# A gated-linear-attention layer with a convolutional FFN on one core: VectorE's order in the opening fixed, side work moved to other units, the last LayerNorm moved behind the first FFN iteration

## The chip, the cores and the metric

The kernel runs on one core of one Trainium2 chip. Its metric is the device time of one execution in microseconds (us). Three runs of the kernel before took 2148.79, 2154.12 and 2155.0 us; their median is 2154.12 us. The execution that the profiler recorded took 2152.2 us.

## What is computed

One decoder layer on 2048 tokens of width 1024, in float32. First a token mixer, gated linear attention in 4 heads (key width 128, value width 256, chunks of 64 tokens), then a gated FFN (inner width 2816) with a causal depthwise convolution of width 3. Each of the two is modulated by a conditioning vector c (shift, scale, gate) and followed by a residual and a LayerNorm:

```python
cs = jax.nn.silu(c)
shift, scale, gate = jnp.split((cs @ w_mod + b_mod)[:, None, :], 3, axis=-1)
y = sublayer(x * (1 + scale) + shift)
x = layer_norm(DN_ALPHA * x + (1 + gate) * y, ln_gain, ln_bias)
# sublayer 1
q, k, v, r, a_lr = jnp.split(h @ w_in, [qk, 2 * qk, 2 * qk + dv, 2 * qk + 2 * dv], axis=-1)
log_a = jax.nn.log_sigmoid((a_lr @ w_a2 + b_a).astype(jnp.float32)) / GLA_TAU
# S_t = diag(a_t) S_(t-1) + k_t^T v_t, o_t = q_t S_t, then norm, * silu(r), @ w_o
# sublayer 2
u, g = jnp.split(h @ w_up, 2, axis=-1)
return (jax.nn.silu(conv(u)) * g) @ w_down
```

## The kernel before

Every float32 operand of a matmul is split into a high and a low part, x = hi + lo. The high part is a cast by ScalarE (ACT, L107), the low part a subtraction by VectorE (DVE, L110). A product is three matmuls of TensorE (PE): hi·hi, hi·lo, lo·hi (mm3, L113 to L115). So each tile that PE is to multiply passes ScalarE and VectorE first.

The program has these stages, by the trace: the opening (0 to 60.6 us), four token blocks of 512 tokens each for the mixer (to 875.9 us), 44 iterations of the FFN's up product (22 column groups for each of two halves of the tokens), and the down product, which ends at 2142.1 us; a tail follows.

*Opening.* Shift and scale for x are needed first. For each pair pr of k-tiles (two tiles of 128 of the 1024 input channels), VectorE sums c-weighted rows of the modulation matrix (mod_cols: one pass of ScalarE and seven of VectorE over macc, L233), four small matmuls against ones turn the sum into a column (mod_fin, L242), and VectorE adds the bias (md, L243). Then x of this pair is modulated (make, L529), split into xm, and multiplied with the weight units of q, k, v and with the decay weights (waw, L508 and L509). A weight unit is 512 KB of raw weights, split into a tile hl. Until then PE runs matmuls on a constant tile (spin, L423).

*Token blocks.* A block goes through units of weights; at_unit(u, f) runs a side step f when unit u is taken. Such side steps are gate_step (a column of a gate, summed over rows by VectorE), x_pre (sums of tokens for the FFN), make_xm (modulating x of the next block, L385), next_decays, ln1_out (LayerNorm output, transposed) and the first weights of the FFN. Heads are worked in pairs: K is scaled by decays into KI (L637) and decayed again by VectorE (L641), PE transposes it (L658), and then multiplies Q with KI and v with the transposed KTt. After the block follows out_proj (L753) with its LayerNorm: bn_stats and bn_aggr on VectorE, one over the root on POOL (L173, L174, L802), the normalisation on ScalarE (normalise, L803).

*FFN.* The up product is done by seven products of sums of tiles (prod), like Strassen's. x for these lies in tiles xc, weights are summed on VectorE (L319). A result in PSUM is copied out by ScalarE (keep: p1, u2, u3; L941) before the next product of the same bank may change it, so a late copy holds up PE.

*Tail.* The last down product ends with an eviction by VectorE, the sum of squares by ScalarE (L1186), one over the root on POOL (L1193, L1194) and two rounds of y (L1191, L1197), then the stores.

A scheduler sets the order of each engine's instructions when the program is built; order(a, b) fixes that a comes after b on the same engine, without a wait. An engine runs its instructions strictly in that order, so one that waits holds up all behind it. DMAs are issued by SyncE's queue (SP).

## Time and profile before

| | before |
|---|---|
| median of three runs | 2154.12 us |
| profiled execution | 2152.2 us |
| its span, first to last instruction | 2150.5 us |
| mean granted TensorE clock | 0.997 |
| PE busy | 2129.3 us (99%) |
| VectorE busy | 1428.9 us (66%) |
| ScalarE busy | 890.3 us (41%) |
| POOL busy | 116.9 us (5%) |

Busy time is time in which an engine ran instructions. PE's matmuls are pipelined, so a record of 0.39 us follows another after about 0.23 us. A row of the timeline gives the start, the time and the instruction, with xN where N equal ones follow each other; the bracket at the end is the idle time before it and what ended it. The granted clock is a share of TensorE's full speed of 2.4 GHz.

### The profile page before, as it was taken

The numbers are of one execution on the slowest core, as the hardware profiler recorded it, in microseconds if no ns is written. First come the engines' busy times: TensorE is split into PE (matmuls) and PEld (weight loads), VectorE is DVE, ScalarE is ACT, GpSimd is POOL, SyncE is SP. The second block draws the span as 40 slices with busy tenths as digits, with TensorE's granted clock in tenths as the row PEclk, the third lists the DMA queues.
The fourth block names the chain that finished last, engine by engine and source line by source line (L and its number), as shares of the span: only waits on it lengthen the run. The fifth ranks groups of instructions, "written<-read, shape, count | busy, mean of one in ns | idle before, by whom it ended". The sixth has DMA issues, their size and how long they took to land.

```text
span 2150.5 us, 26695 instructions
## 1 busy us (share of the span) xinstructions
PE 2129.3 (99%) x9909; PEld 1773.2 (82%) x9909; DVE 1428.9 (66%) x2001; ACT 890.3 (41%) x1346; POOL 116.9 (5%) x266
## 2 busy tenths in 40 slices
PE   9999999999999999999999999999999999999998
PEld 7888888888888888788888888888888888888886
DVE  7786676434743453777877778776666796578556
ACT  4655443424242333644444445333333443344333
POOL 0010100010001000100000000000000000021002
PEclk9999999999999999999999999999999999999999
DMA  8386887674866666767845559877777797577562
GB/s 301 117 320 218 321 324 275 220 252 174 294 228 254 250 237 231 268 225 283 313 175 185 184 210 326 307 256 265 258 270 266 270 333 262 194 239 257 192 203 88
DMA packets 154818, 529.28 MB, mean 246 GB/s; under 512 B 17632, under 2 KB 21856, under 8 KB 134464
## 3 DMA queue, kind: packets, MB, share of 16 engines
q1 hardware_dynamic: 154688, 527.58, 69.0%
q8 instruction: 78, 1.28, 0.2%
q14 instruction: 52, 0.43, 0.1%
HBM read 364.72 MB, written 162.79 MB: 245 GB/s over the span
## 4 chain that ended last, share of the span: by engine, by line
PE 91%; DMA 3%; DVE 2%; ACT 1%; issue 1%; POOL 0%; SPq 0%; DVEq 0%; POOLq 0%; ACTq 0%
PE ps_mm L113 22%; PE ps_mm L115 22%; PE ps_mm L114 22%; PE ps_w L114 8%; PE ps_w L113 8%; PE ps_w L115 8%; DMA mraw<-in_mws_dram 1%; PE ps_w L786 1%; PE ps_w L738 1%; DMA xs<-xm_d 0%; DMA xraw<-in_xT_dram 0%; DMA xs<-xt_d 0%; DMA graw<-in_mwg_dram 0%; PE ps_w L508 0%; DMA xp<-xm_d 0%
## 5 line engine op out<-in xcount | busy, mean ns | idle before, releaser
L113 PE MATMUL ps_mm<-xc,hl 128*128 128x512 f32 x704 | 274.5, 390 | 2.0 <-ACT hl L107 1.9
L115 PE MATMUL ps_mm<-xc,hl 128*128 128x512 f32 x704 | 274.3, 390 | 0.5 <-DVE hl L110 0.5
L114 PE MATMUL ps_mm<-xc,hl 128*128 128x512 f32 x704 | 274.1, 389 | 0.0
L113 PE MATMUL ps_mm<-xm,hl 128*128 128x512 f32 x496 | 194.9, 393 | 1.4 <-DVE v L110 1.4
L114 PE MATMUL ps_mm<-xm,hl 128*128 128x512 f32 x496 | 193.6, 390 | 0.0
L115 PE MATMUL ps_mm<-xm,hl 128*128 128x512 f32 x496 | 193.6, 390 | 0.0
L113 PEld LDWEIGHTS ps_mm<-xc,hl 128*128 128x128 f32 x704 | 132.3, 188 | 29.9 <-ACT hl L107 2.4
L115 PEld LDWEIGHTS ps_mm<-xc,hl 128*128 128x128 f32 x704 | 132.2, 188 | 28.5 <-DVE hl L110 1.0
L114 PEld LDWEIGHTS ps_mm<-xc,hl 128*128 128x128 f32 x704 | 132.2, 188 | 27.7 <-DVE xc L110 0.5
L955 DVE SCALAR_TENSOR_TENSOR ct<-U,cw_sb,ct 128x512 f32<-128x512 f32 x176 | 131.8, 749 | 19.3 <-ACT ct L949 17.8
L115 PE MATMUL ps_w<-xc,hl 128*128 128x512 f32 x352 | 136.9, 389 | 0.0
L113 PE MATMUL ps_w<-xc,hl 128*128 128x512 f32 x352 | 136.9, 389 | 0.0
L114 PE MATMUL ps_w<-xc,hl 128*128 128x512 f32 x352 | 136.9, 389 | 0.0
L107 ACT CAST dhl<-raw 128x1024 fp32r<-128x1024 f32 x57 | 60.2, 1056 | 165.6 <-PE ps_mm L115 101.5
L110 DVE TENSOR_TENSOR dhl<-raw,dhl 128x1024 fp32r<-128x1024 f32 x57 | 69.7, 1223 | 70.1 <-ACT dhl L107 70.1
L113 PEld LDWEIGHTS ps_mm<-xm,hl 128*128 128x128 f32 x496 | 93.2, 188 | 20.7 <-DVE v L110 1.8
L115 PEld LDWEIGHTS ps_mm<-xm,hl 128*128 128x128 f32 x496 | 93.2, 188 | 19.8 <-issue 0.2
L114 PEld LDWEIGHTS ps_mm<-xm,hl 128*128 128x128 f32 x496 | 93.3, 188 | 18.2 <-issue 0.2
L107 ACT CAST hl<-raw 128x1024 fp32r<-128x1024 f32 (+1 forms) x73 | 70.6, 969 | 88.4 <-PE ps_mm L115 41.2
L110 DVE TENSOR_TENSOR hl<-raw,hl 128x1024 fp32r<-128x1024 f32 (+1 forms) x73 | 81.4, 1117 | 36.6 <-ACT hl L107 36.0
L113 PE MATMUL ps_mm<-dhl 128*128 128x512 f32 x264 | 102.7, 389 | 0.0
L114 PE MATMUL ps_mm<-dhl 128*128 128x512 f32 x264 | 102.7, 389 | 0.0
(237 smaller groups left out, 4960.3 us busy)
## 6 DMA issues: line engine op xcount, KB each, us to landing
hl<-wq_d SPq DMA_DIRECT2D x82, 1024.0 KB, 4.9
hc_d<-ct SPq DMA_DIRECT2D x154, 256.0 KB, 2.7
raw<-hc_d SPq DMA_DIRECT2D x70, 512.0 KB, 4.3
draw<-wc_d SPq DMA_DIRECT2D x70, 512.0 KB, 4.7
wq_d<-hl SPq DMA_DIRECT2D x32, 1024.0 KB, 4.9
raw<-in_wab_dram SPq DMA_DIRECT2D x46, 512.0 KB, 6.4
wu<-in_wup_dram SPq DMA_DIRECT2D x44, 512.0 KB, 4.3
wg<-in_wup_dram SPq DMA_DIRECT2D x44, 512.0 KB, 3.7
```

Source lines behind the costliest of these rows:

```text
L107: accs["copy"] = nc.scalar.copy(h, src)
L110: return nc.vector.tensor_tensor(l, src if lsrc is None else lsrc, h.bitcast(F32), op=ALU.subtract)
L113: nc.tensor.matmul(po, a[0], b[0], start=first, stop=False, skip_group_check=resumed)
L114: nc.tensor.matmul(po, a[0], b[1], start=False, stop=False, skip_group_check=resumed)
L115: return nc.tensor.matmul(po, a[1], b[0], start=False, stop=last, skip_group_check=resumed)
L738: nc.tensor.transpose(pt[:, s * P:s * P + P], on[:, s, e * P:e * P + P], ident)
L786: nc.tensor.transpose(pt[:, t * P:t * P + P], src, ident)
L955: nc.vector.scalar_tensor_tensor(ct, U[:, o + i:o + i + 512], cw_sb[:, j, i:i + 1], ct, op0=ALU.mult, op1=ALU.add)
```

## The change

1. Opening: a list (seq) puts every VectorE instruction of the opening in one fixed order. The high parts of x come directly from ScalarE's modulating pass; VectorE computes the low part. For even k-tiles VectorE modulates a copy (xr) itself, for odd ones ScalarE makes a second pass. Two weight units are loaded ahead of x and not one. Each pair's products come in the order q and k, v, mod_fin of the next pair, decays. Twelve spin matmuls stand ahead of the second mod_fin.
2. gate_step of the first block is placed at units 10 to 15 and gate_end at 16, before at 12 to 19 and 20.
3. The modulation of the next block's x (make_xm) is ordered behind the latest decay pass on K.
4. In the last block x_pre comes at units 1 and 12 of the block, before at 4 and 13; the LayerNorm output of block 2 is read back from DRAM at units 14 to 17 of block 3.
5. Start of the FFN: one x tile is loaded at unit 25 of block 3, the others come in halves, two of them later; the last block's LayerNorm is written behind the first iteration.
6. Tail: the last LayerNorm takes bn_stats and bn_aggr (VectorE) and no sum of squares by ScalarE.

```diff
-SPIN = (64, 13)
+SPIN = (64, 8, 12)
...
-    def mod_fin(s, pr):
+    def mod_fin(s, pr, stand_in=None):
         acc = accs.pop((s, pr))
         pm = psum("w", 4)
+        if stand_in is not None:
+            stand_in(pm)
...
-                    nc.vector.tensor_scalar(r, r, md[:, 0, kt, 1:2], md[:, 0, kt, 0:1], op0=ALU.mult, op1=ALU.add)
+                    i = nc.vector.tensor_scalar(r, r, md[:, 0, kt, 1:2], md[:, 0, kt, 0:1], op0=ALU.mult, op1=ALU.add)
+                    order(i, accs["k"])
...
+        def seq(i):
+            if dve:
+                order(i, dve[-1])
+            dve.append(i)
+            return i
...
-        mod_cols(0, 0, range(4), start[0][0])
+        mod_cols(0, 0, range(4), start[0][0], seq=seq)
...
             def make(pr):
-                mm, i = mod_fin(0, pr)
+                mm, i = mod_fin(0, pr, (lambda pm: spin(SPIN[2], pm)) if pr == 1 else None)
+                seq(i)
                 if pr == 0:
-                    order(i, accs["hl"])
                     spin(SPIN[1], ps_spin, mm)
+                    seq(accs["hl"])
                 for kt in (2 * pr, 2 * pr + 1):
                     r = start[pr][1][:, kt % 2 * 512:kt % 2 * 512 + 512]
-                    if kt == 1:
-                        i = nc.vector.tensor_scalar(r, r, md[:, 0, kt, 1:2], md[:, 0, kt, 0:1], op0=ALU.mult, op1=ALU.add)
+                    t = act_tile("xm")
+                    b, a = md[:, 0, kt, 0:1], md[:, 0, kt, 1:2]
+                    hi = nc.scalar.activation(t[:, 0], r, AF.Identity, bias=b, scale=a)
+                    if kt % 2 == 0:
+                        rr = t2p.tile([P, 512], F32, tag="t2", name="xr")
+                        seq(nc.vector.tensor_scalar(rr, r, a, b, op0=ALU.mult, op1=ALU.add))
                     else:
-                        nc.scalar.activation(r, r, AF.Identity, bias=md[:, 0, kt, 0:1], scale=md[:, 0, kt, 1:2])
-                    if kt == 1:
-                        fw.append(unit())
-                        order(accs["hl"], i)
-                    t = act_tile("xm")
-                    sub = split(t[:, 0], t[:, 1], r)
+                        rr = r
+                        hi = nc.scalar.activation(r, r, AF.Identity, bias=b, scale=a)
+                    seq(nc.vector.tensor_tensor(t[:, 1], rr, t[:, 0].bitcast(F32), op=ALU.subtract))
                     xm.append(t)
-                return sub
+                return hi
...
             fw.append(unit())
-            done = make(0)
-            mod_row1(0, 1, start[1][0], accs["copy"])
-            accs["last"] = done
-            make_waw(done)
-            issue(3)
+            seq(accs["hl"])
+            fw.append(unit())
+            hi = make(0)
+            mod_row1(0, 1, start[1][0], hi)
+            split_unit(3, hi)
+            decay_w = make_waw()
+            hi = next(decay_w)
             for pr in range(4):
                 if pr < 3:
                     load_unit()
                     if pr < 2:
                         start_loads(pr + 2)
-                        mod_row1(0, pr + 2, start[pr + 2][0], accs["copy"])
-                    mod_cols(0, pr + 1, range(4), start[pr + 1][0], range(1, KT), accs["hl"] if pr == 0 else mod_done)
-                    mod_done = accs["last"]
-                for po, w in ((pq, fw[0]), (pk, fw[1])):
-                    wv = w.rearrange("p s (k c) -> p s k c", k=KT)
-                    for kt in (2 * pr, 2 * pr + 1):
-                        mm3(po, (wv[:, 0, kt], wv[:, 1, kt]), (xm[kt][:, 0], xm[kt][:, 1]), kt == 0, kt == KT - 1)
+                        mod_row1(0, pr + 2, start[pr + 2][0], hi)
+                    mod_cols(0, pr + 1, range(4), start[pr + 1][0], range(1, KT), seq)
+                if pr == 0:
+                    next(decay_w, None)
+                kts = (2 * pr, 2 * pr + 1)
+                views = [(po, w.rearrange("p s (k c) -> p s k c", k=KT)) for po, w in ((pq, fw[0]), (pk, fw[1]))]
+
+                def part(kt, a, b):
+                    for po, wv in views:
+                        nc.tensor.matmul(po, wv[:, a, kt], xm[kt][:, b], start=kt + a + b == 0,
+                                         stop=kt == KT - 1 and b == 1)
+
+                for kt in kts:
+                    part(kt, 0, 0)
+                    part(kt, 1, 0)
+                    if pr > 0:
+                        part(kt, 0, 1)
+                if pr == 0:
+                    for kt in kts:
+                        part(kt, 0, 1)
+                v_part(banks, pr, xm, pr == 0)
                 if pr < 3:
-                    accs["last"] = make(pr + 1)
-                mm_a(pa, xm, (2 * pr, 2 * pr + 1))
+                    hi = make(pr + 1)
+                    split_unit(4 + pr, hi)
+                mm_a(pa, xm, kts)
                 if pr == 2:
                     make_w2s()
-                if pr < 3:
-                    issue(4 + pr)
-                v_part(banks, pr, xm)
...
-            nc.vector.tensor_tensor(kk, kk, el[:, 1:3].rearrange("p c s -> p s c")[:, :, :, None].to_broadcast([P, 4, 2, CH]),
-                                    op=ALU.mult)
+            d = el[:, 1:3].rearrange("p c s -> p s c")[:, :, :, None].to_broadcast([P, 4, 2, CH])
+            accs["k"] = nc.vector.tensor_tensor(kk, kk, d, op=ALU.mult)
...
-                if half == 1:
-                    normalise(zs[t])
-                    store(zn_d[tb * 4 + t], zs[t])
+                if half == 1 and tb < NTB - 1:
+                    ln1(tb, t, zs)
             tick()
+
+        def ln1(tb, t, zs):
+            normalise(zs[t])
+            store(zn_d[tb * 4 + t], zs[t])
...
+            first["x"] = [raw_tile("xs") for pr in range(2)]
+            for pr in range(2):
+                load(first["x"][pr], xt_d[0][3][pr])
...
-                for k in range(8):
-                    at_unit(12 + k, gate_step, 0, k, gs1)
-                at_unit(20, gate_end, 0, G1, gs1)
+                for k, u in enumerate((10, 10, 11, 11, 11, 12, 14, 15)):
+                    at_unit(u, gate_step, 0, k, gs1)
+                at_unit(16, gate_end, 0, G1, gs1)
...
-                at_unit(b + 4, x_pre, 0, 0)
-                at_unit(b + 13, x_pre, 0, 1)
+                at_unit(b + 1, x_pre, 0, 0)
+                at_unit(b + 12, x_pre, 0, 1)
+                for pr in range(4):
+                    at_unit(b + 14 + pr, ln1_out, 2, None, (pr,))
...
-            if 0 < tb < NTB - 1:
+            if tb == 1:
...
+        def x_halves(i):
+            X0[i] = []
+            for pr in range(2):
+                t = x_tile(ur, i)
+                half, b = X_AT[i] if i < 4 else (0, 0)
+                for k in range(2):
+                    r = hid_tile("xs")
+                    load(r, xm2_d[b][2 * half + pr][:, k] if i < 3 else xt_d[0][i][pr][:, k * 512:k * 512 + 512])
+                    h = t[:, :, k * 512:k * 512 + 512]
+                    split(h[:, 0], h[:, 1], r)
+                    X0[i].append((h[:, 0], h[:, 1]))
+
+        x_halves(4)
...
-            if n == 0:
-                start_rest()
...
+            if n == 0:
+                x_fill(ur, X0, 3, first["x"])
...
+            if n == 0:
+                x_halves(2)
+                for t in range(4):
+                    ln1(NTB - 1, t, zs_last)
...
+    def ln2_last(p, b, t):
+        a, sm = acc.pop((p, b, t))
+        st = sts.pop()
+        nc.vector.bn_stats(st[:, 1], a[:, 512:1024])
+        mv = smp.tile([P, 2], F32, tag="mv", name="mv")
+        nc.vector.bn_aggr(mv, st)
+        rs = smp.tile([P, 2], F32, tag="rs", name="rs")
+        rsqrt_eps(rs[:, 0:1], mv[:, 1:2])
...
+            y = t2p.tile([P, 512], F32, tag="t2", name="y")
+            nc.vector.scalar_tensor_tensor(y, a[:, cs_], mv[:, 0:1], rows[2][half], op0=ALU.subtract, op1=ALU.mult)
...
+            nc.vector.scalar_tensor_tensor(ys[half], ys[half], rs[:, 0:1], rows[3][half], op0=ALU.mult, op1=ALU.add)
...
-                    ln2(p, b, t)
+                    ln2_last(p, b, t)
...
+                    sts.append(smp.tile([P, 2, 6], F32, tag="bst", name="bst"))
+                    nc.vector.bn_stats(sts[-1][:, 0], acc[p, b, t][0][:, 0:512])
```

How this moves instructions shows in the order of the two programs at three places. First VectorE in the opening, from the md of the second pair to that of the third; macc is the sum of modulation rows, xm the split x, hl a weight unit. Before:

```order
L243 TENSOR_TENSOR md<-ps_w,mbs_sb 128x4
L233 SCALAR_TENSOR_TENSOR macc<-mraw,cs,macc 128x512 x3
L110 TENSOR_TENSOR xm<-xraw,xm 128x512 x2
L233 SCALAR_TENSOR_TENSOR macc<-mraw,cs,macc 128x512
L110 TENSOR_TENSOR hl<-raw,hl 128x1024
L233 SCALAR_TENSOR_TENSOR macc<-mraw,cs,macc 128x512 x2
L243 TENSOR_TENSOR md<-ps_w,mbs_sb 128x4
```

and after the change, where xr is the modulated copy:

```order
L244 TENSOR_TENSOR md<-ps_w,mbs_sb 128x4
L556 TENSOR_SCALAR xr<-xraw,md 128x512
L560 TENSOR_TENSOR xm<-xr,xm 128x512
L560 TENSOR_TENSOR xm<-xraw,xm 128x512
L110 TENSOR_TENSOR hl<-raw,hl 128x1024
L233 SCALAR_TENSOR_TENSOR macc<-mraw,cs,macc 128x512 x7
L244 TENSOR_TENSOR md<-ps_w,mbs_sb 128x4
```

The passes over macc were spread around the splits of x and of the weights; now all splits of a pair stand in front of all seven passes for the next one. On PE, at the end of the second pair's work, before (L242 is mod_fin, hl,xm the v product):

```order
L115 MATMUL ps_mm<-hl,xm 128x512
L113 MATMUL ps_mm<-hl,xm 128x512
L242 MATMUL ps_w<-ones,macc 128x1 x4
L114 MATMUL ps_mm<-hl,xm 128x512
L115 MATMUL ps_mm<-hl,xm 128x512
```

and after (L243 is mod_fin, L521 and L522 the decay matmuls, L591 the next pair's q and k):

```order
L115 MATMUL ps_mm<-hl,xm 128x512
L522 MATMUL ps_w<-xm,waw 96x512
L521 MATMUL ps_w<-xm,waw 96x512
L522 MATMUL ps_w<-xm,waw 96x512
L243 MATMUL ps_w<-ones,macc 128x1 x4
L591 MATMUL ps_w<-xm,hl 128x512 x12
L113 MATMUL ps_mm<-hl,xm 128x512 x4
```

mod_fin stood among the v products of its pair and now stands behind the last matmul of the pair.

Second, the first head, on PE: behind the Q·KI matmuls, before:

```order
L114 MATMUL ps_w<-Q,KI 128x192
L115 MATMUL ps_w<-Q,KI 128x192
L114 MATMUL ps_mm<-xm,hl 128x512
L115 MATMUL ps_mm<-xm,hl 128x512
L113 MATMUL ps_mm<-xm,hl 128x512
```

and after:

```order
L114 MATMUL ps_w<-Q,KI 128x192
L115 MATMUL ps_w<-Q,KI 128x192
L113 MATMUL ps_w<-v,KTt 128x256
L114 MATMUL ps_w<-v,KTt 128x256
L115 MATMUL ps_w<-v,KTt 128x256
```

The product of v with KTt followed later and now follows at once. VectorE from the decay pass of the first head (KI_787) to KTt, after:

```order
L684 TENSOR_TENSOR KI_787<-KI_787,el 128x512
L667 SCALAR_TENSOR_TENSOR Q_823<-ps_mm,E_772 128x4x64
L110 TENSOR_TENSOR KI<-KI_860,KI 128x512
L668 TENSOR_TENSOR Q_823<-Q_823,el 128x4x64
L684 TENSOR_TENSOR KI_860<-KI_860,el 128x512
L110 TENSOR_TENSOR Q<-Q_823,Q 128x768
L110 TENSOR_TENSOR KTt<-ps_w,KTt 128x512
```

Six instructions stand from there to KTt's low part, one of them (KI of the second head, KI_860) in front of the second head's decay pass.

Third, ScalarE at the start of the FFN, where z is a LayerNorm tile, hl a weight unit, p1 and u2 are copies from PSUM and xc is x, before:

```order
L803 ACTIVATE z_7262<-z_7262,rs_7570 128x1024
L107 CAST h3_7616<-s3_7504 128x512
L803 ACTIVATE z_7264<-z_7264,rs_7582 128x1024
L107 CAST hl_7662<-wg_7345 128x1024
L941 COPY p1_7657<-ps_mm_7644 128x512
L803 ACTIVATE z_7266<-z_7266,rs_7594 128x1024
L803 ACTIVATE z_7268<-z_7268,rs_7606 128x1024
L107 CAST hl_7703<-wu_7640 128x1024
L941 COPY u2_7720<-ps_mm_7644 128x512
L107 CAST hl_7725<-wu_7640 128x1024
```

and after:

```order
L107 CAST hl_7653<-wg_7376 128x1024
L993 COPY p1_7648<-ps_mm_7635 128x512
L107 CAST xc_7611<-xs_7612 128x512
L107 CAST xc_7611<-xs_7616 128x512
L848 ACTIVATE z_7295<-z_7295,rs_7772 128x1024
L107 CAST xc_7620<-xs_7621 128x512
L107 CAST hl_7674<-wu_7631 128x1024
L107 CAST xc_7620<-xs_7625 128x512
L1001 ACTIVATE ct_7672<-U_7669,cb_sb_104,cw_sb_103 128x512
L107 CAST xc_7677<-xs_7379 128x1024
L107 CAST xc_7680<-xs_7380 128x1024
L993 COPY u2_7697<-ps_mm_7635 128x512
```

Two LayerNorm passes stand ahead of the cast of hl (hl_7703 before, hl_7674 now; the first of the two above these rows) where four stood, and the copy of u2, which followed it at once, now has three more casts and a convolution pass ahead of it.

## Rows read from the trace of the kernel before

**Rows 1.** The page's part 1: busy time, share, instructions of each engine.

```profile
PE 2129.3 (99%) x9909; PEld 1773.2 (82%) x9909; DVE 1428.9 (66%) x2001; ACT 890.3 (41%) x1346; POOL 116.9 (5%) x266
```

**Rows 2.** Waits of PE: engine line waited for, total us, times, longest us.

```profile
PE ps_w L658 <- DVE KI L641: 3.0, 3, 1.3
...
PE ps_mm L113 <- ACT hl L107: 1.9, 1, 1.9
PE ps_mm L113 <- DVE v L110: 1.4, 1, 1.4
...
PE ps_w L113 <- ACT v L107: 0.3, 1, 0.3
PE ps_w L114 <- DVE v L110: 0.3, 1, 0.3
```

**Rows 3.** Timeline, PE, opening: start us, us, engine line op, idle before.

```profile
15.53 0.73 PE L113 MATMUL ps_w<-xm,hl 128*128 128x512 f32 x2 [1.19 <-ACT xm L107]
...
24.68 1.05 PE L242 MATMUL ps_w<-ones,macc 128*128 128x1 f32 x8 [0.35 <-DVE macc L233]
...
28.50 1.22 PE L113 MATMUL ps_w<-xm,hl 128*128 128x512 f32 x2 [1.76 <-ACT xm L107]
...
60.59 0.63 PE L482 MATMUL ps_w<-A,w2s 96*128 96x512 f32 x2
```

**Rows 4.** Timeline, VectorE (DVE), opening.

```profile
26.23 0.16 DVE L243 TENSOR_TENSOR md<-ps_w,mbs_sb 128x4 f32<-128x4 f32 x1
26.35 2.33 DVE L233 SCALAR_TENSOR_TENSOR macc<-mraw,cs,macc 128x512 f32<-128x512 f32 x3
28.59 1.29 DVE L110 TENSOR_TENSOR xm<-xraw,xm 128x512 fp32r<-128x512 f32 x2
...
30.46 1.22 DVE L110 TENSOR_TENSOR hl<-raw,hl 128x1024 fp32r<-128x1024 f32 x1
```

**Rows 5.** Timeline, ScalarE (ACT), opening.

```profile
26.42 1.52 ACT L539 ACTIVATE xraw<-xraw,md 128x512 f32<-128x512 f32 x2 [0.89 <-DVE md L243]
```

**Rows 6.** Windows: us, busy (x) of PE, PEld, DVE, ACT, POOL, granted clock, DMA, GB/s.

```profile
24.20:27.70 3.50, 2.19 (x13) 1.46 (x12) 2.53 (x5) 2.00 (x3) 0.00 (x0) 1.00 1.05 414
27.70:34.60 6.90, 6.10 (x14) 4.63 (x15) 5.36 (x8) 2.94 (x5) 0.00 (x0) 0.51 1.04 409
34.60:60.60 26.00, 26.00 (x124) 21.45 (x123) 17.16 (x23) 12.98 (x18) 0.00 (x0) 1.00 0.61 209
128.00:131.90 3.90, 2.72 (x12) 1.90 (x11) 3.90 (x6) 3.90 (x8) 0.51 (x3) 1.00 0.98 350
...
884.00:887.80 3.80, 1.41 (x6) 0.52 (x4) 1.20 (x1) 2.99 (x4) 0.27 (x1) 1.00 0.69 267
887.80:891.40 3.60, 3.52 (x8) 2.84 (x9) 2.42 (x4) 2.09 (x3) 0.00 (x0) 0.53 1.06 288
```

**Rows 7.** Timeline, PE, first head.

```profile
75.34 0.65 PE L658 MATMUL ps_w<-ident,KI 128*128 128x128 f32 x4 [0.92 <-DVE KI L641]
...
77.15 0.42 PE L114 MATMUL ps_mm<-xm,hl 128*128 128x512 f32 x1
```

**Rows 8.** Timeline, VectorE, first head.

```profile
77.64 0.96 DVE L110 TENSOR_TENSOR Q<-Q,Q 128x768 fp32r<-128x768 f32 x1
...
79.12 0.68 DVE L110 TENSOR_TENSOR KTt<-ps_w,KTt 128x512 fp32r<-128x512 f32 x1
```

**Rows 9.** Timeline, VectorE, third token block.

```profile
588.21 0.55 DVE L385 TENSOR_SCALAR xraw<-xraw,md 128x512 f32<-128x512 f32 x1 [0.22 <-DMA xraw<-in_xT_dram]
```

**Rows 10.** Timeline, ScalarE, start of the FFN.

```profile
885.54 1.03 ACT L107 CAST hl<-wu 128x1024 fp32r<-128x1024 f32 x1
```

**Rows 11.** Timeline, POOL, start of the FFN.

```profile
881.46 1.59 POOL L802 TENSOR_SCALAR rs<-mv,rs 128x1 f32<-128x1 f32 x1
```

**Rows 12.** Timeline, VectorE, end.

```profile
2143.46 1.42 DVE L1191 SCALAR_TENSOR_TENSOR y<-acc,lsm,row 128x512 f32<-128x512 f32 x2 [0.62 <-POOL lsm L1184]
2145.66 1.41 DVE L1197 SCALAR_TENSOR_TENSOR y<-y,lsm,row 128x512 f32<-128x512 f32 x2 [0.79 <-POOL lsm L1194]
```

More of the change, by code (lines that the diff above doesn't have):

```diff
@@ L215, in mod_row1, with mod_cols @@
         order(nc.scalar.activation(accs[s, pr], mod_row(raws, 0), AF.Copy, scale=cs[:, 0:1]), after)
-    def mod_cols(s, pr, qs, raws=None, rows=range(KT), after=None):
+    def mod_cols(s, pr, qs, raws=None, rows=range(KT), seq=None):
         if raws is None:
@@ L447, in make_w2s @@
             load(w2r, wa2)
-            order(nc.scalar.copy(w2s, w2r), accs["last"])
-            nc.vector.tensor_tensor(w2s[64:96], w2r[64:96], w2s[64:96].bitcast(F32), op=ALU.subtract)
+            order(nc.scalar.copy(w2s, w2r), dve[-1])
+            seq(nc.vector.tensor_tensor(w2s[64:96], w2r[64:96], w2s[64:96].bitcast(F32), op=ALU.subtract))
         smask = ab.tile([P, TB], F32, name="smask")
@@ L897 @@
             out_proj(tb, 1, gated, zs, tick)
-            if not last:
+            if last:
+                zs_last = zs
+            else:
                 xm = nxt["xm"]
@@ L1110 @@
             hid_late()
+            if n == 0:
+                x_halves(2)
+                for t in range(4):
+                    ln1(NTB - 1, t, zs_last)
             for f, *a in todo.pop(n, ()):
```

50 lines of the change are left out of this document (29 added, 21 removed).

## The prediction

> **What bounds the kernel now.** The page's first part comes first: TensorE (PE) is busy 2129.3 of the 2150.5 us of the span, 99% [rows 1]. No other engine can be the bound of the whole, and an edit pays only where it removes idle time of PE, about 21 us in all (2150.5 - 2129.3), or time at the lower clock. Second, the view of waits, for PE alone, says who ends that idle time [rows 2]: VectorE's decayed keys (KI) 3.0 us in three waits, one weight split (hl) by ScalarE 1.9 us, VectorE's low part of v 1.4 us, and two small waits for v of 0.3 us each. Third, the timeline of the opening [rows 3 to 5] shows PE waiting for modulated x (xm) twice, 1.19 and 1.76 us. Fourth, the view of windows gives the granted clock [rows 6]: it is 1.00 (2.4 GHz) nearly everywhere, but 0.51 from 27.7 to 34.6 us and 0.53 from 887.8 to 891.4 us (1.2 GHz for practically all of it). PE had been busy 2.19 of 3.5 us before the first fall and 1.41 of 3.8 us before the second; 2.72 of 3.9 us ahead of 131.9 us had no such consequence. Work done at half the clock takes twice its time, so the two stretches cost half of their busy time: 6.10/2 = 3.05 us and 3.52/2 = 1.76 us. All that this change can touch is thus some 15 us: small waits at six places, and these two stretches.
>
> **The change part by part.** I count a gain as plus, against the profiled execution.
>
> *Opening, pairs 1 to 3.* Before, the eight passes over macc ahead of the second pair's md include one that belongs to the pair after (x8 against x7 in the order). Without it md comes 0.78 us (2.33/3) earlier than 26.39 (26.23 + 0.16), at 25.6 [rows 4]. The high half of xm then comes straight from the first ScalarE pass, 0.76 us (1.52/2) [rows 5], where before two passes and two casts stood; so this pair's matmuls can start at 26.4 and not at 28.50 [rows 3]. But the order of PE takes something back: mod_fin's four matmuls used to stand in the middle of a pair's work, and now stand behind all of it. PE work of one pair is 40 long matmuls. In 34.6 to 60.6 us 124 records took 26.0 us [rows 6]; 16 of them are two mod_fins (8 records, 1.05 us each [rows 3]), so a long one is (26.0 - 2.1)/108 = 0.22 us and a pair 8.9 us. To this come 1.05 (mod_fin), 0.16 (md) and 0.76 (high half): a period of 10.9 us in which PE has nothing to do for 0.16 + 0.76 us plus what mod_fin and its latency leave, about 2 us. VectorE's own chain of a pair, now in one fixed line, is 0.16 + 0.65 + 1.29 + 1.22 + 7 x 0.78 [rows 4] + 1.05 = 9.8 us, and about 0.4 us more since its second subtraction waits for three ScalarE passes (2.3 us); with semaphores between two or three engines I put the period at 10.9 to 11.3. Starts are then 26.4, 37.5 and 48.6, and the opening ends at 57.6 instead of 60.59 [rows 3]: +3.0 at the full clock. Two idle times of 2 us may each lower the clock. I charge one fall at the smaller price, 1.76 us, since the idle time before that one (1.9 us [rows 2]) is of the size of these: **+1.2**, bounds 3.0 - 2 x 3.05 = -3.1 and +3.0. The spare spin matmuls lie in the wait ahead of the second mod_fin (24.68 [rows 3]) and cost nothing as long as that wait is there; else they cost their own 12 matmuls, under 1.5 us.
>
> On the clock the Trainium skill (TensorE: Matmul & The Clock Gate, section "HAM oscillation — how this bites in real kernels") says that a kernel whose PE waits between bursts falls back to the half clock and pays for the transition at every such wait. [...]
>
> *First head.* The KI chain gets one more 512-wide pass ahead of it (0.68 us, as KTt's [rows 8]) and two more matmuls as cover (60 for 58, 0.45 us): **-0.2** on a wait of 0.92 us [rows 7]. Behind it, the state product v·KTt now follows the Q·KI matmuls at once, where 14 others stood between. PE gets there 1.8 us (77.15 - 75.34) after the transposes start [rows 7]. VectorE, from the end of the KI pass that the transposes wait for, has six instructions up to KTt's low half: three 512-wide at 0.68, Q's at 0.96 [rows 8], and two of half that width, each between 0.34 and 0.68. That is 3.7 to 4.4 us; I take 3.8, since a half-wide pass is the nearer to half. A new wait of 3.8 - 1.8: **-2.0** (bounds -2.6 and 0, zero if the pieces reach VectorE in another order than written).
>
> *Gate steps at earlier units.* They take two gate passes and their POOL company from ahead of the v halves, for which PE waited 1.4 us [rows 2]: **+1.0** (0 to 1.4), and v of the last token tile, 0.6 us in two waits [rows 2]: **+0.6**. They load VectorE among the first two heads; no wait of PE stands there now, and I carry -1 as a bound.
>
> *Token sums at v.* In the third token block the modulation of x (L385) waited for its DMA till 588.2 us [rows 9], and KI stood behind it on VectorE. Now these passes are ordered behind the decay. Of the 3.0 us for KI, 0.92 belong to the first head [rows 2, 7], 1.3 to this place, and the rest, 0.8, to the fourth block, where KI stood among the token-sum subtractions that are moved to other units. **+1.3** and **+0.7**. What is late next is x for the following block, first used some units later. The LayerNorm output of block 2 now comes back from DRAM: its loads join SP's queue, at -0.5 at worst.
>
> *Start of the FFN.* Before, ScalarE's cast for the second unit of weights came at 885.54, ended at 886.57 [rows 10], and PE waited 1.9 us for it [rows 2]; with the rest of the idle time of 884 to 887.8 (3.8 - 1.41 = 2.4 us) and 1.76 us of half clock the place cost 4.2 us. It was late because two LayerNorm passes of ScalarE stood ahead of it, and these waited for POOL, one instruction of which took 1.59 us [rows 11]. Afterwards one LayerNorm pass and three half-wide casts (0.5 us each, half of 1.03) stand ahead of that cast, so it starts between 884.5 and 885.5. PE has 12 other matmuls (2.7 us) to do first. But the u2 copy, which the product after them needs, is now behind this cast, another half-wide one, a conv pass (0.8, as the pass of [rows 5]) and two full casts (2 x 1.03): 4.4 us after the cast's start, 888.9 to 889.9, plus 0.6 for the copy itself. PE would be there at 884.7 (886.6 less 1.9) + 2.7 = 887.4. It waits 2.1 to 3.1 us, and the clock falls as before: **0**, bounds -2 (POOL slow once more) and +4.2 (no wait left).
>
> POOL's 1.59 us stands in a stretch in which VectorE subtracts. The Trainium skill (SBUF — State Buffer, section "SBUF: two separate sides") says that a VectorE operation with two SBUF inputs and a GpSimd operation exclude each other for a whole instruction. By it this step would again be slow, as split subtractions fill that stretch, and the term would be -2 and not 0.
>
> *End.* The two y passes start at 2143.46, and the second two wait until 2145.66 for ScalarE's sum of squares and POOL [rows 12]. With bn_stats there is one more 512-wide pass and an aggregation before (0.2 us net, as two small POOL steps go), the wait of 2145.66 - 2143.46 - 1.42 = 0.78 us goes: **+0.5** (-0.3 to +0.8).
>
> The sum: 1.2 - 0.2 - 2.0 + 1.0 + 0.6 + 1.3 + 0.7 + 0 + 0.5 = 3.1 us. The profiled execution took 2152.2 us, 1.9 below the median of the runs, 2154.12. So 2149.1 against the one and 2151.0 against the other; I forecast 2150.
>
> **Rivals.**
> 1. *All of it is hidden.* The bubbles of the opening keep the clock (+3.0), KTt isn't waited for, KI's wait goes (+0.9), v +2.0, the other KI waits +2.0, the FFN starts without a wait (+4.2), the end +0.5: 12.6 at most, I say 11: 2141 to 2143. For it: each wait is small and the removed work stands in front of each. Against: the orders of PE and ScalarE show two new places where a producer stands too close.
> 2. *The change doesn't do what it says.* The last LayerNorm is meant behind the first FFN iteration, yet its four passes still stand on ScalarE within that iteration, and the opening's gain is eaten by its bubbles. Then only small terms of either sign remain: 2152 to 2154.
> 3. *Slower, by the clock.* Each new idle stretch of about 2 us or more (two in the opening, one at KTt) is followed by half clock at the price of 27.7 to 34.6, 3.05 us. Opening 57.6 + 6.1 = 63.7: -3.1. KTt -2.0 - 3.05 = -5.1. The FFN start falls for a second stretch: -1.8. Against these +1.0 + 0.6 + 1.3 + 0.7 + 0.5 - 0.2 = 3.9: 6.1 slower, 2158 to 2160. It decides if the clock is near 0.5 behind at least three of these places. For it speak the two falls [rows 6], against it the stretch 128 to 131.9, with 1.2 us idle and no fall.
>
> **How the numbers follow.** Forecast 0.46, rival 1 0.25, rival 2 0.12, rival 3 0.17. What a measurement of this kernel can tell from no change is about 0.3%, 6.5 us: under 2147.7 is faster, over 2160.6 slower. Faster: nearly all of rival 1 (0.24) and 0.12 of the forecast, whose switch and KTt terms could both come out near their better ends. Slower: 0.11 of rival 3, 0.02 of the others. The rest is the same: 0.51. The range goes from inside rival 1 to inside rival 3, 2142 to 2159; the forecast's own is 2146 to 2154.
>
> **What would show it.** Opening: PE's mod_fin matmuls at the end of a pair's work, idle time of about 2 us ahead of pairs 2 and 3, and the opening's last matmul between 57 and 60 us. First head: a wait of L113 ps_w for KTt of 2 us. No waits for KI near 592 and 713, none over 0.5 for v near 132. FFN start: PE waits for ScalarE's u2 or xc and not for hl. End: the last two y passes follow the first two without a gap. The forecast is wrong if the clock stays at 1.00 through both places (then rival 1), or if PE waits at places that don't wait now.

## The result, and the profile after

The median after the change is 2167.88 us (2167.36 to 2170.89), against 2153.74 us (2148.79 to 2155.0) before: a ratio of 1.0073, 95% interval 1.0054 to 1.0091. The kernel became slower by 14 us between the medians and 16 us between the profiled executions, outside the predicted range and beyond the slowest rival. The profiled execution after took 2168.27 us, its span is 2166.5 us, 16.0 more than before, at a mean granted clock of 0.995.

The first part of the page (busy time, share of the span and instructions of each engine), after:

```profile
PE 2134.0 (99%) x9916; PEld 1775.3 (82%) x9916; DVE 1434.8 (66%) x2018; ACT 883.2 (41%) x1337; POOL 119.2 (6%) x258
```

PE is busy 4.7 us longer than in [rows 1] and idle 32.5 us (2166.5 - 2134.0), where it was 21.2. The waits of PE after (engine, line waited for, total us, times, longest):

```profile
PE ps_mm L113 <- DMA hl<-wq_d: 5.7, 1, 5.7
PE ps_w L831 <- DMA zc<-zn_d: 3.5, 3, 1.6
PE ps_w L591 <- ACT xm L553: 2.8, 3, 1.1
PE ps_mm L113 <- ACT hl L107: 2.1, 1, 2.1
...
PE ps_w L700 <- DVE KI L684: 1.1, 1, 1.1
...
...
PE ps_mm L113 <- DVE v L110: 0.8, 1, 0.8
PE ps_w L113 <- ACT KTt L107: 0.6, 1, 0.6
PE ps_w L115 <- DVE KTt L110: 0.6, 1, 0.6
```

Against [rows 2], KI went from 3.0 to 1.1 us, v from 1.4 to 0.8, and the FFN's wait for hl (1.9) is gone. The two largest lines are new, and both name a DMA: a weight unit read back from wq_d, and zc, the LayerNorm output of block 2 read back from zn_d. The line for hl by ScalarE is now another place, as the timeline of PE shows (start us, us, instruction, idle before and what ended it):

```profile
38.63 0.73 PE L591 MATMUL ps_w<-xm,hl 128*128 128x512 f32 x2 [1.10 <-ACT xm L553]
...
79.36 0.66 PE L700 MATMUL ps_w<-ident,KI 128*128 128x128 f32 x4 [1.06 <-DVE KI L684]
...
81.97 0.38 PE L113 MATMUL ps_w<-v,KTt 128*128 128x256 f32 x1 [0.64 <-ACT KTt L107]
...
216.78 0.65 PE L113 MATMUL ps_mm<-hl,gated 128*128 128x512 f32 x1 [2.11 <-ACT hl L107]
219.17 0.79 PE L114 MATMUL ps_mm<-hl,gated 128*128 128x512 f32 x1 [0.89 <-DVE hl L110]
...
702.22 0.77 PE L113 MATMUL ps_mm<-xm,hl 128*128 128x512 f32 x1 [5.74 <-DMA hl<-wq_d]
...
806.48 0.41 PE L831 MATMUL ps_w<-ident,zc 128*128 128x128 f32 x2 [1.56 <-DMA zc<-zn_d]
```

The windows give the granted clock there (us, busy of PE, PEld, DVE, ACT, POOL, clock, DMA share, GB/s):

```profile
39.40:42.90 3.50, 3.50 (x10) 2.73 (x9) 2.50 (x3) 1.66 (x2) 0.00 (x0) 0.51 0.06 26
...
217.00:223.80 6.80, 5.91 (x14) 4.02 (x14) 6.80 (x8) 1.59 (x2) 0.00 (x0) 0.50 0.81 327
697.90:701.70 3.80, 0.00 (x0) 0.00 (x0) 0.00 (x0) 0.00 (x0) 0.00 (x0) 0.99 0.99 388
701.70:705.10 3.40, 2.88 (x7) 2.35 (x8) 0.00 (x0) 0.00 (x0) 0.00 (x0) 0.50 1.00 424
...
906.50:909.90 3.40, 3.40 (x10) 2.63 (x9) 3.40 (x6) 3.22 (x5) 1.37 (x2) 0.50 0.42 158
```

While PE had work, four stretches ran at 1.2 GHz where [rows 6] have two. For 3.8 us before 701.7 all five engines stood still while the DMA engines were 99% busy; PE waited for a load.

Matmul by matmul (each against its counterpart in the other profile), with the half clock counted in, the two profiles part as follows (gain is plus). Each profile is one execution.

| place | predicted | measured |
|---|---|---|
| opening, to the matmul behind it (60.84 against 60.59) | +1.2 | -0.2 |
| first head, KI and KTt | -2.2 | -1.9 |
| v, 131 to 169 us | +1.6 | +1.8 |
| behind the gate steps, 216 to 224 us | 0, bound -1 | -5.6 |
| token sums, 592 us | +1.3 | +1.4 |
| 702 us (5.9 lost, then 2.9 us of work at half clock) | at most -0.5, | -7.3 |
| zc, 779 to 809 us (1.4, 0.9, 1.7, 0.4) | with this | -4.4 |
| KI, 713 us | +0.7 | +0.9 |
| start of the FFN | 0 | +0.2 |
| FFN later (a wait at 1061.75) | none | -0.7 |
| end | +0.5 | +0.3 |

The measured column sums to -15.5 of the 16.0 us. The gate steps' stall and the two DMA waits of the fourth block are 17.3 us of loss, where the prediction had at most 1.5.

### The profile page after: what moved, and what is told of

Read it like the earlier page. It is cut to its first block, busy times and chain, and to the rows that moved or that the text cites. A ratio compares the mean times of both kernels' runs of the same rounds, so it can differ in the third digit from the quotient of the medians.

```text
span 2166.5 us, 26743 instructions
## 1 busy us (share of the span) xinstructions
PE 2134.0 (99%) x9916; PEld 1775.3 (82%) x9916; DVE 1434.8 (66%) x2018; ACT 883.2 (41%) x1337; POOL 119.2 (6%) x258
## 4 chain that ended last, share of the span: by engine, by line
PE 88%; DMA 4%; DVE 3%; ACT 2%; issue 1%; POOL 0%; SPq 0%; DVEq 0%; POOLq 0%
PE ps_mm L113 21%; PE ps_mm L114 21%; PE ps_mm L115 21%; PE ps_w L115 7%; PE ps_w L114 7%; PE ps_w L113 7%; DMA xp<-xm_d 1%; DMA xraw<-in_xT_dram 1%; DMA raw<-in_wab_dram 1%; DMA mraw<-in_mws_dram 1%; PE ps_w L831 1%; DMA hl<-wq_d 1%; PE ps_w L591 0%; PE ps_w L780 0%; DMA zc<-zn_d 0%
## 5 line engine op out<-in xcount | busy, mean ns | idle before, releaser
L113 PE MATMUL ps_mm<-hl,gated 128*128 128x512 f32 x256 | 101.0, 394 | 2.1 <-ACT hl L107 2.1
L115 PE MATMUL ps_mm<-dhl 128*128 128x512 f32 x264 | 102.7, 389 | 0.0
```

The source lines that it names most:

```text
L113: nc.tensor.matmul(po, a[0], b[0], start=first, stop=False, skip_group_check=resumed)
L115: return nc.tensor.matmul(po, a[1], b[0], start=False, stop=last, skip_group_check=resumed)
```

## Experiments

**The fourth block.** block3_back takes back the units of x_pre and the reading of zc:

```diff
-at_unit(b + 1, x_pre, 0, 0)
-at_unit(b + 12, x_pre, 0, 1)
-for pr in range(4):
-    at_unit(b + 14 + pr, ln1_out, 2, None, (pr,))
+at_unit(b + 4, x_pre, 0, 0)
+at_unit(b + 13, x_pre, 0, 1)
 ...
-if tb == 1:
+if 0 < tb < NTB - 1:
```

> The changed kernel with the side work of the fourth token block put back: token sums at units 4 and 13, LayerNorm output of block 2 from SBUF at units 2 and 3. Theory (queue): the block's two new kinds of waits, one weight load 5.7 us late with 1.7 us of half clock behind it and three waits of 3.5 us in all for zc, come from SyncE's queue and go; the KI wait of 0.9 us near 713 comes back: 2157 us, 10 to 11 below the changed kernel's 2167.9, and no wait of PE for a DMA. Rival (opening): the late start of the first block shifts all that follows and the waits appear elsewhere in the block: 2164 or more.

Measured: 2159.85 us, ratio 1.0043 (1.0026 to 1.0060). A ratio is always to the kernel before, estimated from all runs, and need not be the quotient of two medians. No wait of PE for a DMA is left. So these lines cost about 0.3 points of the 0.73%, each ratio being known to some 0.2. One expectation failed: the wait for KI near 713 us did not come back, although x_pre stands at its old units.

sums_late takes back only the two units of x_pre; stores_late leaves x_pre at unit 1 but issues its four stores three units later, behind the weight loads:

```diff
-at_unit(b + 1, x_pre, 0, 0)
+at_unit(b + 1, x_pre, 0, 0, b + 4)
 ...
+def put():
+    for m, r in ((4, b11), (6, b12), (5, b22), (3, b21)):
+        order(store(xt_d[hf][m][pr], r), stream_loads[-1])
+at_unit(later, put)
```

> The changed kernel with the token sums at units 4 and 13 of the fourth block again, LayerNorm output of block 2 still read back from DRAM at units 14 to 17. Queue theory: the 5.7 us wait for hl near 702 goes and with it the half clock; the zc waits stay within 2 us of 4.4: 2160 to 2161 us. Rival (it is the reading back of zn that clogs the queue): the wait at 702 stays, 2166 or more.

> The changed kernel with only the four stores of the first token sums put off: loads and sums stay at unit 1 of the fourth block, the stores stand behind the weight loads of unit 4. Theory (order in SyncE's queue): the weight load waits because it stands behind stores that wait for VectorE's sums; with the stores behind it the load leaves before 690 us and PE's wait of 5.7 us goes: 2160 to 2161 us. Rival (bandwidth): the four loads of 512 KB beside the weights are what makes the weight late; the wait stays above 3 us: 2165 or more.

Measured: sums_late 2162.3 us, 1.0045 (1.0028 to 1.0062); stores_late 2159.64 us, 1.0040 (1.0025 to 1.0055). In both the 5.7 us are gone and 2.6 us of waiting for zc stay in two waits; the times of the three kernels are too close to price zc apart. SyncE's queue in the changed kernel (start and time of the issue; xp are tokens for the sums, xt_d the sums):

```profile
680.31 0.41 SPq L136 DMA_DIRECT2D hl<-wq_d  x1
680.81 2.46 SPq L271 DMA_DIRECT2D xp<-xm_d  x4
690.28 0.32 SPq L279 DMA_DIRECT2D xt_d<-xp  x1
...
694.23 0.32 SPq L285 DMA_DIRECT2D xt_d<-xp  x1
694.65 2.26 SPq L136 DMA_DIRECT2D hl<-wq_d  x4
```

and in stores_late:

```profile
680.40 2.46 SPq L271 DMA_DIRECT2D xp<-xm_d  x4
682.91 8.06 SPq L136 DMA_DIRECT2D hl<-wq_d  x3
691.07 3.53 SPq L285 DMA_DIRECT2D xt_d<-xp  x4
```

With the change the next weight load is issued 14.3 us after the one before (694.65 - 680.31). VectorE makes the four sums only when xp has landed, and the queue stands at the first store until then (a row of VectorE's timeline, and one of the queue's waits between 660 and 720 us, both after the change):

```profile
689.03 5.17 DVE L277 TENSOR_TENSOR xp<-xp 128x1024 f32<-128x1024 f32 x4 [12.25 <-DMA xp<-xm_d]
...
SPq L279 <- DVE xp L277: 7.0, 1, 7.0
```

With the same transfers in another order the load goes at 682.91. So it is the order of the queue, not the amount of data.

**The gate steps.** gate_back puts them at units 12 to 19 and 20 again; gate_steps_alone is the kernel before with nothing but the earlier units (its edit is shown):

```diff
-for k in range(8):
-    at_unit(12 + k, gate_step, 0, k, gs1)
-at_unit(20, gate_end, 0, G1, gs1)
+for k, u in enumerate((10, 10, 11, 11, 11, 12, 14, 15)):
+    at_unit(u, gate_step, 0, k, gs1)
+at_unit(16, gate_end, 0, G1, gs1)
```

> The changed kernel with the gate steps of the first block back at units 12 to 19 and 20. Theory (first block's waits at 216 us come from VectorE and SyncE being late in a circle: x of the next block is loaded behind a weight store that waits for VectorE, and VectorE waits for that x): gate steps are not its start, the waits for hl near 217 to 220 stay at 3 to 4 us, and the wait for v near 133 goes from 0.8 back to 1.4: 2168 to 2169 us. Rival (the gate steps' moved loads start the circle): the waits near 217 fall under 1 us and the half clock behind them goes: 2162 us.

> The kernel before with the gate steps of the first block at the earlier units and nothing else changed. Theory (the early gate steps keep the raw buffers occupied, the weight loads of 145 to 165 us come one by one and everything behind them late): a wait of PE for ScalarE's and VectorE's hl near 216 us of 2 us or more and half clock there, the wait for v near 132 us 0.6 us shorter; 2153.5 to 2157. Rival (only together with the earlier loads of the opening do they collide): no wait over 0.6 us near 216, 2149 to 2151.

Measured: gate_back 2164.81 us, 1.0062 (1.0047 to 1.0077), without the stall at 216 us; the theory that the gate steps are not its start was wrong, and the time lies between the two expectations. gate_steps_alone: 2157.59 us against 2150.03, 1.0032 (1.0020 to 1.0045). By themselves they make the kernel 7 us slower, and the stall is there in its timeline of PE:

```profile
207.24 0.50 PE L113 MATMUL ps_mm<-hl,gated 128*128 128x512 f32 x1 [1.14 <-ACT gated L107]
215.70 0.50 PE L113 MATMUL ps_mm<-hl,gated 128*128 128x512 f32 x1 [2.46 <-ACT hl L107]
218.56 0.79 PE L114 MATMUL ps_mm<-hl,gated 128*128 128x512 f32 x1 [1.90 <-DVE hl L110]
```

The way there starts 70 us earlier. Loads of raw weights on SyncE's queue, before:

```profile
146.12 3.01 SPq L128 DMA_DIRECT2D raw<-in_wab_dram  x4
```

and after:

```profile
144.65 0.33 SPq L147 DMA_DIRECT2D wq_d<-hl  x1
145.07 0.38 SPq L128 DMA_DIRECT2D raw<-in_wab_dram  x1
...
149.33 0.42 SPq L128 DMA_DIRECT2D raw<-in_wab_dram  x1
...
154.81 1.73 SPq L128 DMA_DIRECT2D raw<-in_wab_dram  x1
...
165.00 0.43 SPq L128 DMA_DIRECT2D raw<-in_wab_dram  x1
```

The gate steps' rows go into the same pool of four raw tiles as weights and x. With the steps late, four loads go in one burst (gate_back shows it too, from 146.39 on); with the steps early they go one by one, in gate_steps_alone as well. Each of the single loads stands right behind a store of a split weight (wq_d), as the first two rows show, where before four loads stood behind one store (at 145.69). The queue's waits between 120 and 216 us, after, are mostly at these stores:

```profile
SPq L147 <- DVE hl L110: 56.5, 8, 11.0
SPq L128 <- DVE xm L110: 9.0, 4, 6.6
```

Before, these two are 52.0 us in ten waits and 5.5 us in four. All behind the loads is late, up to x for the next block, for which VectorE waits, after:

```profile
182.41 1.00 DVE L386 TENSOR_SCALAR xraw<-xraw,md 128x512 f32<-128x512 f32 x2 [4.51 <-DMA xraw<-in_xT_dram]
...
205.92 1.01 DVE L386 TENSOR_SCALAR xraw<-xraw,md 128x512 f32<-128x512 f32 x2 [8.33 <-DMA xraw<-in_xT_dram]
```

and before:

```profile
179.71 1.00 DVE L385 TENSOR_SCALAR xraw<-xraw,md 128x512 f32<-128x512 f32 x2
...
201.62 1.00 DVE L385 TENSOR_SCALAR xraw<-xraw,md 128x512 f32<-128x512 f32 x2 [7.25 <-DMA xraw<-in_xT_dram]
```

VectorE waited for the second x before the change too; what is new is that this pass comes 4.3 us later. With it VectorE's passes over the output weights are late, and PE waits at 216.78. That the units are the cause is shown by both runs. The steps between are read from the traces: whether the loads are late because no raw tile is free, or because they stand behind stores that wait for VectorE, as in the fourth block, is not shown. Neither a larger pool nor another order of the stores was tried.

**What is left.** block3_gate_back takes back both of these parts, so that opening, token sums, FFN start and end remain:

> The changed kernel with the side work of the fourth block and the gate steps both put back. If the two are the whole loss and add up: 216 us waits gone (5.8 us with the half clock), 702 and zc waits gone: 2148 to 2151 us, ratio to before 0.998 to 1.000, PE at matmul 1000 within 0.5 us of the kernel before and 1.4 us ahead from the third block on. Rival (the opening and the first head cost more than 2 us of their own): still slower than before by 2 to 5 us, 2153 to 2156.

Measured: 2152.37 us against 2150.64, 1.0004 (0.9995 to 1.0013): between the two expectations, no difference from before that can be told. Three kernels then add one part each to the kernel before: the opening; the order of VectorE's x passes behind the decay, with the tail; the start of the FFN. Their edits are those parts of the diff above.

> The kernel before with only the new opening. By the traces so far the opening's last matmul comes within 0.5 us of before, either side, depending on whether one bubble lowers the clock; the first head then waits 1.6 us more (KTt) and is made up by nothing: 2151 to 2154, ratio 1.000 to 1.001. Rival (the opening is a gain that the later stalls only hid): 2147 to 2149.

> The kernel before with only the modulation of x ordered behind the decays, and the new last LayerNorm. Theory: the wait of 1.3 us near 592 goes and the end is 0.3 us shorter: 1.5 to 1.8 us faster, 2149 us, ratio 0.9992. Rival (the wait at 592 only went because the changed kernel runs at another phase): no wait removed, ratio 1.000.

> The kernel before with only the new start of the FFN (x tile fetched early, halves, last LayerNorm written behind the first iteration). Theory: a wait of PE for ScalarE (u2, xc) of 2 to 3 us takes the place of the wait for hl of 1.9 us and the half clock follows again: within 1 us of before, 2150 to 2152. Rival (the start is a gain of its own): no half clock at 888 to 891, 2147 to 2148.

Measured: the opening 2154.43 us, 1.0019 (1.0011 to 1.0028), slower by 4 us, a miss; decay order and tail 2148.9 us, 0.9994 (0.9985 to 1.0003), with no wait for KI at 592 us and one of 0.9 us left near 713; the FFN start 2152.05 us, 1.0003 (0.9994 to 1.0012), nothing. With the gate steps (+0.32%) and the fourth block (0.30 points) the single ratios sum to 0.78%, near the 0.73% of the whole change. That each part is worth the same in every kernel is not shown: the gate steps put back take 0.11 points off the changed kernel and 0.39 off block3_back, which their intervals of about 0.2 hardly tell apart, and the traces have their stall at 8.5 us in gate_steps_alone and 5.6 us in the changed kernel.

**Why the opening loses.** The kernels from here on have the decay order and the tail too. opening_spread fills VectorE's waits with macc passes and puts mod_fin ahead of the decays; opening_spread_first_head also moves PE's first-head matmuls behind others; opening_spread_head_ffn adds the FFN start.

```diff
+def late_work(dk):                  # in pairs 1 and 2, after macc pass dk
+    if dk == 1: seq(<second subtraction of xm>)
+    elif dk == 3: seq(<low part of hl>)
 ...
-mm_a(pa, xm, kts)
+mm_a(pa, xm, kts, accs["mm"])       # decays behind mod_fin
 ...
+order(<first transpose of KI>, <third of eight products of the next unit>)
+order(<first v,KTt>, <last product of that unit>)
```

> The kernel before with the decay order and the tail of the change, and with its opening changed in two ways: mod_fin is ordered ahead of the four decay matmuls of its pair instead of behind them, and VectorE's passes over macc fill its waits for ScalarE (one between the two subtractions of xm, two ahead of the split of hl). Theory (PE's two bubbles of 1.24 us come from mod_fin at the end of the pair together with VectorE's unbroken chain md, xr, xm, hl, macc): idle time ahead of pairs 2 and 3 is under 0.5 us each, the granted clock stays at 1.00 between 34 and 60 us, the last matmul of the opening is at 57 to 58.5 us; the waits for KTt (0.7 and 0.6 us) stay; time 2147 to 2149.5. Rival (VectorE's own work of a pair sets the period, so PE only waits for macc instead of xm): the idle time comes back ahead of mod_fin, opening end 59.5 or later, 2151 to 2153.

> The same, with PE's order changed in the first head: the transposes of KI stand behind seven more matmuls of the other product, and the state product of v and KTt behind 15 of them. Theory (the waits for KI, 1.1 us, and for KTt, 1.3 us, are a matter of PE's order alone): both gone, 2.4 us less than the kernel without this change: 2144.5 to 2147. Rival (the later products hold back what VectorE does next, so the wait comes back at the second head or at out_proj): less than 1 us gained, a new wait of PE between 85 and 135 us.

> The same, and the start of the FFN as the change has it. Theory (that part alone is worth nothing): within 1 us of the kernel without it, 2144.5 to 2147.5, its waits at 884 to 894 us for u2 and xc in place of the one for hl. Rival (with the rest of the work further ahead it meets another state of the loads): over 2148.5.

Measured: 2152.67 us (1.0011, 1.0002 to 1.0020), 2153.14 us (1.0015, 1.0006 to 1.0024) and 2152.5 us (1.0007, 0.9998 to 1.0015), all against 2150.03. All three times are those of the rivals. In the first the bubbles of xm are gone and the opening keeps the full clock, but PE waits 0.93 and 0.94 us for the low part of hl instead (not for macc, as the rival had it); in the second the waits for KI and KTt shrink and this appears on PE, with half clock behind it:

```profile
88.71 0.46 PE L113 MATMUL ps_w<-Q,KI 128*128 128x192 f32 x1 [2.53 <-DVE KTt L110]
```

A wait that can be moved but not removed may have its cause elsewhere. VectorE in the first head, before (mn is the first step of the decays):

```profile
62.02 0.74 DVE L489 TENSOR_SCALAR mn<-ps_w,ba_sb 128x512 f32<-128x512 f32 x1
...
74.60 0.68 DVE L641 TENSOR_TENSOR KI<-KI,el 128x512 f32<-128x512 f32 x1
```

and after:

```profile
65.20 0.75 DVE L502 TENSOR_SCALAR mn<-ps_w,ba_sb 128x512 f32<-128x512 f32 x1 [1.36 <-ACT az L498]
...
78.62 0.68 DVE L684 TENSOR_TENSOR KI<-KI,el 128x512 f32<-128x512 f32 x1
```

The whole chain is 3 to 4 us later although the opening ends at the same time: in the last pair the change puts the decay matmuls behind v, and the decays are what the first head starts with. last_pair has the change's opening with these four, and their eviction, in front again; spread_last_pair adds the spreading, spread_last_pair_ffn the FFN start too:

```diff
+if pr == 3:
+    mm_a(pa, xm, kts)
 v_part(banks, pr, xm, pr == 0)
 if pr < 3:
     hi = make(pr + 1)
     split_unit(4 + pr, hi)
-mm_a(pa, xm, kts)
+    mm_a(pa, xm, kts)
 ...
+A3 = evac_a(pa)
 v = evac_v(banks)
```

> The kernel before with the decay order, the tail and the opening of the change, but in the last pair of the opening the four decay matmuls stand ahead of the v products again, and their eviction ahead of v's. Theory (the decays of the last pair behind v make VectorE's whole chain of the first head 4 us late: mn at 65.2 us where it was 62.0, the decay pass of KI at 78.6 where it was 74.6; that is what takes PE's cover away): mn starts at 62 to 63 us, the decay pass of KI at 74.5 to 75.5, no wait for KTt over 0.2 us, lag against before of under 0.5 us at 135 us where the opening alone had 1.3: 2147 to 2150. Rival (VectorE's own work bounds the first heads whatever the start): a wait of 1 us or more comes back at the second head, 2151 to 2154.

> As the kernel before this one, with the passes over macc spread between VectorE's subtractions and mod_fin ahead of the decays in pairs 1 and 2 as well. Theory (both losses of the opening, the bubbles and the late decays, are gone): the first-head waits as in the other; PE still waits 1.1 us twice for the split of hl, which the spreading made late; 2147 to 2149.5. Rival: the same as for the other, 2151 to 2153.

> The same with the start of the FFN as the change has it, so all of the change but the gate steps and the fourth block, with both losses of the opening taken out. Theory: within 1 us of the kernel before it in this list, 2146.5 to 2149.5. Rival: over 2150.5.

Measured, against 2150.63 us: 2151.64 (0.9999, 0.9990 to 1.0008), 2150.4 (0.9992, 0.9983 to 1.0002) and 2149.74 (0.9995, 0.9986 to 1.0004). VectorE in last_pair:

```profile
60.44 0.74 DVE L502 TENSOR_SCALAR mn<-ps_w,ba_sb 128x512 f32<-128x512 f32 x1
...
72.61 0.68 DVE L687 TENSOR_TENSOR KI<-KI,el 128x512 f32<-128x512 f32 x1
```

and PE:

```profile
73.34 0.66 PE L703 MATMUL ps_w<-ident,KI 128*128 128x128 f32 x4 [0.93 <-DVE KI L687]
...
78.40 0.28 PE L113 MATMUL ps_w<-v,KTt 128*128 128x256 f32 x1
```

The chain is 5 to 6 us earlier than after the change, the v·KTt matmuls stand behind fourteen others again, and nothing waits for KTt. Some 2 us of this are PE's own, since this execution's opening had no half clock and ended that much earlier; the rest, 3.8 us at the decay pass, is the order. From the end of the opening to behind the first head, PE loses 1.9 us against the kernel before in all seven traces with the change's opening and first head, and nothing in last_pair. So the late decays, not VectorE's amount of work, cause the loss of the first head; the order of the matmuls and that of the eviction were not tried apart. This is about half of the 4 us that the opening alone costs. The rest lies in the opening itself and is not resolved: last_pair is 0.20 points below opening_alone, of which decay order and tail, which it has besides, are 0.06.

The medians lie 0.2 to 1.6 us above what was expected; that of last_pair lies in its rival's range, but the wait at the second head that the rival names did not come. No version is shown to beat the kernel before, as each of the three intervals reaches 1, like that of decay_order_and_tail. The bubble ahead of pairs 2 and 3 is in last_pair still, 1.10 us each, at the full clock.

## Why the prediction was wrong

*The fourth block is the step that failed most.* The prediction says of the LayerNorm output that "its loads join SP's queue, at -0.5 at worst", and costs x_pre's new place by VectorE's passes alone. Measured are -4.4 and -7.3. Four loads and four stores go with each x_pre, and the stores wait for VectorE; the prediction names SP's queue and does not follow what stands behind them: a weight load that goes at 694.65 us, and at 682.91 when the stores stand behind it (stores_late). The waits for zc are there in every run that reads it back from DRAM in this block and in none that takes it from SBUF (block3_back, block3_gate_back). Its only evidence would have been a row of SyncE's queue in block 4, and no row of [rows 1 to 12] is one.

*Gate steps.* "no wait of PE stands there now, and I carry -1 as a bound": measured -5.6, far behind the steps, at the output weights of the block. The gain that was forecast for v, 1.6, came (1.8). What was missed again is transfers: eight loads that share raw tiles and queue with the weights.

*Opening.* +1.2 against -0.2 up to its end. The two idle stretches stood ahead of pairs 2 and 3 as forecast (36.5 to 38.63 and 49.5 to 51.53 us), with one fall of the clock as charged. But md of the second pair, forecast at 25.6, came at 26.20, hardly earlier than before: VectorE's passes over macc ended at 24.81, and mod_fin, behind the twelve spin matmuls, started at 25.22. So the second pair began at 27.27 and not at 26.4, and the period was 11.4 us and, with the half clock, 12.9.

That the clock fell once is luck. The same opening ran without a fall in gate_back, which ended it 1.6 us ahead of the kernel before, and with two in stores_late and block3_gate_back, which ended it 1.1 and 1.8 us behind. The kernel before varies as well: its profiled execution has 6.9 us at half clock in the opening, and three kernels with the same opening (gate_steps_alone, decay_order_and_tail, ffn_start_alone) have 3.4 us and end it 1.1 to 1.9 us earlier. The -0.2 is thus one draw, and against those three the new opening does worse on average. The larger error is in the next step.

*First head.* -2.2 forecast, -1.9 measured, with KTt's waits (0.64 and 0.61 us) where they were expected: the size was right, the cause wrong. The prediction counts "60 for 58" matmuls of cover ahead of the transposes and lets VectorE be 0.68 us later. The trace has 16 more matmuls ahead of them (the transposes are number 268 where they were 252), and VectorE 4.0 us later, by the decays of the last pair. Had the order of PE at the end of the opening been read down to its last pair, this would have been seen as a loss that one edit avoids (last_pair).

*Token sums, start of the FFN, end* came out as forecast: 1.4 for 1.3, 0.2 for 0, 0.3 for 0.5. *KI in block 4* has the right size, 0.9 for 0.7, but not the reason given: with x_pre back at its old units (block3_back, sums_late, block3_gate_back) no wait for KI is left near 713 either, and decay order, opening or FFN start alone each leave one of 0.6 to 1.0 us. What removes it stays open. At the FFN's start PE indeed waits for xc (0.22 and 0.85 us) and u (1.00) and no longer for hl, and the clock falls at 906.5.

*The rivals.* The slower one was right in sign and wrong in mechanism: it had the clock fall behind the waits that the prediction knew. Half clock is in the loss (1.75 us at 39.4, 3.0 at 217, 1.4 at 701.7, half of PE's busy time in each), but the second and third stand behind waits that it did not know. The sign was against the forecast because every place was examined for the compute engines' order, and the transfers that a moved step issues got no more than a bound of 0.5 us.

Of the clock, the Trainium skill (TensorE: Matmul & The Clock Gate, section "HAM oscillation — how this bites in real kernels") describes a kernel that waits for a DMA behind each burst of matmuls and begins every burst at the half clock; its waits are longer than the bubbles here. The two bubbles of the opening, 1.10 us idle each, are alike in the changed kernel and in last_pair, yet in the first one of two is followed by half clock and in the second none. Kernels with the very same opening had none, one or two falls. A bubble of this length can cost the clock here and need not.

## What to carry to other kernels

A step that is moved takes its DMAs with it: write down what stands behind them in the issuing queue, whether one of them waits for compute, and which pool its buffers come from, before counting engine passes. A wait that only moves when the waiting engine's order is changed has its cause upstream; look for the first instruction of the chain that became late. Where one bubble may or may not lower the clock, compare several executions before a place of 2 us is called a gain or a loss. Keep what starts the next stage ahead of bulk work at a stage's end, even if a loop's other turns want the opposite order.

## What the runs showed of the hardware that was not expected

POOL's small operations are slowed by VectorE passes beside them. One over the root takes two of them in the tail. Before, with nearly all of it behind the first y passes:

```profile
2144.78 0.19 POOL L1193 TENSOR_SCALAR lsm<-lsm 128x1 f32<-128x1 f32 x1 [1.36 <-ACT sq L1186]
2145.05 0.57 POOL L1194 TENSOR_TENSOR lsm<-lsm,mhalf 128x1 f32<-128x1 f32 x1
```

After, where the change lets VectorE's two y passes (1.41 us from 2160.13 on) run beside them:

```profile
2160.18 0.77 POOL L173 TENSOR_SCALAR rs<-mv 128x1 f32<-128x1 f32 x1 [3.31 <-DVE mv L1242]
2161.03 0.93 POOL L174 TENSOR_TENSOR rs<-rs,mhalf 128x1 f32<-128x1 f32 x1
```

0.94 us more for the pair, and the y passes of the second round still wait 0.45 us for it, where 0.78 us of waiting were to go; with that wait left, the end gave 0.3 and not 0.5. The Trainium skill (SBUF — State Buffer, section "SBUF: two separate sides") says that a VectorE operation with two SBUF inputs and a GpSimd operation exclude each other; these rows agree. At the FFN's start after the change L173 and L174 took 1.35 and 1.58 us for two each, and L847 1.33 us for one, beside the split subtractions; beside bn_stats, which reads one tile, L173 and L174 took 0.23 and 0.57 us (at 897.36).
